# A block with 16,384 routed experts on one Trainium2 core: the expert outputs summed with the tokens on the partitions, in six banks held over all 128 tiles

## The chip, the cores and the metric

One core of a Trainium2 chip runs the whole program. The metric is device microseconds of one execution. The kernel before took 2893.17 us (median of three runs, 2893.05 to 2893.21). Five engines run beside each other, each in the order of its own queue: PE (matmuls; its weight loads are listed as PEld), DVE (vector work), ACT (activations and copies), POOL (here the gathers and some products) and SP (here it only issues DMAs). DMA issues stand in the queues of SP, ACT and POOL, and sixteen DMA engines carry them out.

## What is computed

The program is two transformer blocks on one sequence of 512 tokens, 1024 wide, in float32. The first ends in a mixture of 128 x 128 experts ("peer"), and the change lies wholly in that:

```python
def one_block(hb):                       # 128 tokens
    ...
    g = jax.nn.softmax(top_s, axis=-1)   # 8 heads x 16 chosen experts per token
    u = u_tab[idx]
    act = jax.nn.gelu(jnp.einsum('thkd,td->thk', u, hb))
    wts = (g * act.astype(jnp.float32)).astype(hb.dtype)
    v = v_tab[idx]
    return jnp.einsum('thk,thkd->td', wts, v)
```

Both expert tables are 16,384 x 1024. After this come a SwiGLU feed-forward (`f1`), a mixing layer and a second feed-forward.

## The kernel before

Activations lie transposed: eight tiles `x[m]` of 128 features by 512 tokens. Each float32 operand of a product is split into two fp32r parts, `hi` (a rounded copy, made by ACT) and `lo` (the rest, made by DVE), and a product is three matmuls: hi x hi, lo x hi, hi x lo (`mm3`, lines 235 to 237). Weights come through `wchunk`: SP loads 512 KB into one of three `wraw` buffers (line 210), ACT makes `whi` (line 211), DVE makes `wlo` (line 212), three buffers each. In the rows of a product the first name behind the arrow streams through the array, the second is loaded as weights.

The experts (`phase_b`) are computed in two ways. For the first 128 tokens the chosen rows are gathered: POOL issues an indirect DMA per slot (line 924, 128 of `u_nat` and 128 of `v_nat`, 512 KB each, four `row` buffers) and DVE multiplies and sums each row (lines 935 and 942). For the other 384 tokens (`ND`) all experts are computed densely, and a gate that is zero for experts not chosen weighs them. The gates, [12 blocks of 32 tokens, 128, 128, 32], are made with one-hot products on PE and written to DRAM in twelve writes by ACT's queue (line 884).

The dense part works on 128 tiles of 128 experts. `u_tile` multiplies one tile of `u` with the tokens, 24 matmuls of 384 columns, and applies the gelu (line 958). In the first stage, while the routing runs, 68 tiles are computed and written to DRAM (`spill`). The second stage, which the change rewrites, computes the other 60 `u` tiles and all v products. Its unit is a group of four tiles (`v_group`): read the gates of the group (line 989, runs of 512 bytes), read spilled tiles back (line 997), multiply by the gates (line 999; every second tile on POOL, the others on DVE), split into `whi__` and `wlo__` (lines 1002 and 1003), then for each of eight feature tiles m sum four tiles in one PSUM bank, 12 matmuls of 384 columns with the weights `pv` loaded and the weighted activations streaming, and add the bank to `x[m]` on DVE (line 1014). `seq` mixes the groups of spilled tiles and of tiles computed here; a group whose tiles are computed here starts right behind its fourth `u` tile. The last group also feeds `nf`, the norm ahead of the feed-forward (lines 135 to 147).

`weave` lets the gather run beside this at a set rate, and `pace` ties each of its steps to a recent matmul. A scheduler then sets the order within each engine's queue. PSUM has eight banks: two `mm`, two `S`, two `L`, one `T`, one `st`.

Of the kernel before, what the change touches and what calls it, by code (L numbers as in the profile page):

```python
# [7 lines left out]
F32 = mybir.dt.float32  # L8
F32R = mybir.dt.float32r
# [4 lines left out]
AF = mybir.ActivationFunctionType  # L14
OP = mybir.AluOpType
# [7 lines left out]
T = 512  # L23
# [27 lines left out]
GR = 0.45  # L51
RR = 1.1
VR = 0.345
AR = 1.4
MR = 1.75
PT = 12
SO = 0.5
TB = 8
BC = 2600
GSC = 32768.0  # L60
# [110 lines left out]
class Kern:  # L171
# [539 lines left out]
    def phase_b(self, n2):  # L711
        nc, I, x = self.nc, self.I, self.x
        ACT, V, G = nc.scalar, nc.vector, nc.gpsimd
        ND = T - TG
        NTB = ND // 32
        dp = self.ctx.enter_context(self.tc.tile_pool(name="dram", bufs=1, space=DRAM))
        Gd = dp.tile([NTB, 128, 128, 32], F32, name="gates")
        Sd = dp.tile([SPILL, 128, ND], F32, name="spill")
        eg = ExitStack()
        gp_ = eg.enter_context(self.pool("gath", "right"))  # L720
        er = ExitStack()
# [2 lines left out]
        rp = erq.enter_context(self.pool("route", "right"))  # L724
# [43 lines left out]
        rp = er.enter_context(self.pool("route2", "right"))  # L768
# [4 lines left out]
        spilled = {}  # L773
# [137 lines left out]
        def gather():  # L911

            g2 = gsel0.rearrange("p h s -> p (h s)")
            acc = gp_.tile([128, 1024], F32, name="gacc")
            V.memset(acc, 0.0)
            dots = gp_.tile([128, 128], F32, name="dots")
            junk = gp_.tile([128, 1024], F32, name="junk")
# [12 lines left out]
            for n, (tab, s) in enumerate(seq):  # L930
                if n + ROWB - 1 < len(seq):
                    issue(n + ROWB - 1)
                row = rows.pop(n)
                if tab == "u":
                    self.pace(V.scalar_tensor_tensor(junk, row, 1.0, hnat, op0=OP.mult, op1=OP.mult,  # L935
                                                     accum_out=dots[:, s:s + 1]), BACK)
                    if s % 16 == 15:
                        ss = slice(s - 15, s + 1)
                        ACT.activation(dots[:, ss], dots[:, ss], AF.Gelu_apprx_tanh)
                        V.tensor_tensor(dots[:, ss], dots[:, ss], g2[:, ss], op=OP.mult)  # L940
                else:
                    self.pace(V.scalar_tensor_tensor(acc, row, dots[:, s:s + 1], acc, op0=OP.mult, op1=OP.add), BACK)  # L942
                yield 1170
            for k in range(2):
                pt = self.ps("T")
                for q in range(4):
                    m = 4 * k + q
                    nc.tensor.transpose(pt[:, q * 128:(q + 1) * 128], acc[:, m * 128:(m + 1) * 128], self.ident)
                for q in range(4):
                    m = 4 * k + q  # L950
                    V.tensor_tensor(x[m][:, :TG], x[m][:, :TG], pt[:, q * 128:(q + 1) * 128], op=OP.add)
                yield 800

        def u_tile(j, pool, spill):
            ps = self.ps("mm")
            yield from self.proj_g(ps, I["u"][j], hhi, hlo, n=ND, cost=490)
            g = pool.tile([128, ND], F32, name="gs", bufs=3 if spill else 2 * GS)
# [4 lines left out]
            yield 0  # L962

        def u_spill():
            for j in range(SPILL):
                yield from u_tile(j, rp, True)

        gat = gather()

# [14 lines left out]
        ev = ExitStack()  # L984
        vp = ev.enter_context(self.pool("vph", "right"))

        def v_group(g, last):
            gt = vp.tile([128, NTB, GS, 32], F32, name="gt", bufs=2)
            nc.sync.dma_start(gt.rearrange("p a j t -> p a (j t)"),
                              Gd[:, :, g * GS:(g + 1) * GS, :].rearrange("a p j t -> p a (j t)"))  # L990
            W = []
            for q in range(GS):
                j = g * GS + q
                s = spilled[j]
                if s is None:
                    s = vp.tile([128, ND], F32, name="gr", bufs=4)
                    nc.sync.dma_start(s, Sd[j])
                s3 = s.rearrange("p (a t) -> p a t", t=32)
                (G if q % 2 else V).tensor_tensor(s3, s3, gt[:, :, q, :], op=OP.mult)
                a = vp.tile([128, ND], F32R, name="whi_", bufs=2 * GS)  # L1000
                c = vp.tile([128, ND], F32R, name="wlo_", bufs=2 * GS)
                ACT.activation(a, s, AF.Copy)
                V.tensor_tensor(c, s, a.bitcast(F32), op=OP.subtract)
                W.append((a, c))
            for mp in range(4):
                whi, wlo = self.wchunk(I["pv"][g, mp].rearrange("p m j d -> p (m j d)"), 1024)
                for m2 in range(2):
                    m = 2 * mp + m2
                    ps = self.ps("L" if m2 else "S")
                    for q in range(GS):  # L1010
                        o = slice((m2 * GS + q) * 128, (m2 * GS + q + 1) * 128)
# [3 lines left out]
                    if last:  # L1015
                        nf.add(m, x[m])

        nf = Norm(self, "f1")
        sg = list(range(SPILL // GS))
        ug = list(range(SPILL // GS, NG))  # L1020
        seq = []
        ns, nu = len(sg), len(ug)
        a = b = 0
        while a < ns or b < nu:
            if a < ns and (b >= nu or (a + SO) * nu <= b * ns):
                seq.append(sg[a])
                a += 1
            else:
                seq.append(ug[b])
                b += 1  # L1030

        def u_all():
            for g in ug:
                for q in range(GS):
                    yield from u_tile(g * GS + q, vp, False)

        def main():
            ugen = u_all()
            total = nu * GS * 9
            vsteps = NG * GS * 8  # L1040
            done, vdone = 0, 0
            for n, g in enumerate(seq):
                need = (ug.index(g) + 1) * GS * 9 if g in ug else 0
                while done < need:
                    yield next(ugen, 0)
                    done += 1
                if n == len(seq) - 1:
                    yield None
                for c in v_group(g, n == len(seq) - 1):
                    yield c  # L1050
                    vdone += 1
                    while done < total and done * vsteps < vdone * total * 1.08:
                        yield next(ugen, 0)
                        done += 1
            for c in ugen:
                yield c

        weave(main(), gat, VR)
        ev.close()
# [505 lines left out]
def layout(i):  # L1565

    f = lambda n: np.asarray(i[n])
# [33 lines left out]
    r["pv"] = c(f("peer_v")[0].reshape(NG, GS, 128, 4, 2, 128).transpose(0, 3, 2, 4, 1, 5))  # L1601
# [73 lines left out]
```

## Time and profile before

| what | value |
|---|---|
| median of the runs | 2893.17 us |
| profiled execution, its own time | 2896.98 us |
| its span in the trace | 2895.1 us |
| PE busy | 2808.9 us, 97% |
| DVE busy | 2019.7 us, 70% |
| ACT busy | 1159.6 us, 40% |
| POOL busy | 477.1 us, 16% |
| mean granted clock of PE | 0.983 of full speed |

The profiled execution is 3.8 us longer than the median. PE is busy nearly throughout, so a microsecond can come out of PE's own work, out of the gaps in it, or out of stretches at the lower of its two clocks. The second stage of the experts lies between 1101.0 us (the end of the last spilled `u` tile) and 1931.4 us (the end of the last v product), 830.4 us. DVE and the DMA engines are both about nine tenths busy there.

### The profile page before, as it was taken

What the parts mean: (1) busy time and instruction counts of PE and PEld (TensorE: products, weight loads), DVE (VectorE), ACT (ScalarE), POOL (GpSimd) and SP (SyncE); (2) the same over time, 40 slices, a digit from 0 to 9 for tenths busy, and PEclk for the clock granted to TensorE, in tenths of its full rate; (3) what the DMA queues carried; (4) which work ended last, traced back from release to release, by engine and by line L of the source; (5) the groups of instructions that cost most, each with busy time, mean ns of one, the idle gap of its engine ahead of it and who ended that gap; (6) DMA issues with size and microseconds to landing.
All of it is one profiled execution on the core that took longest, in us unless ns stands there. A gap on an engine that the chain in (4) does not pass through costs nothing. (4 is left out here: it accounts for less than half of the span.)

```text
span 2895.1 us, 38874 instructions
## 1 busy us (share of the span) xinstructions
PE 2808.9 (97%) x14613; PEld 2439.5 (84%) x14613; DVE 2019.7 (70%) x3960; ACT 1159.6 (40%) x1723; POOL 477.1 (16%) x352
## 2 busy tenths in 40 slices
PE   8999999999899998999999999999999999999999
PEld 6678777788798898999999999998888877688887
DVE  6753466679999997998898898974443467554432
ACT  5742344333365663333333333343322355633221
POOL 0000000000042334444444444400000000000000
PEclk9999999999999999999999999999999999899999
DMA  4223211332387889988988898832233321132232
GB/s 167 64 77 109 72 52 52 98 108 79 110 302 247 322 296 363 319 308 304 316 293 310 315 307 296 299 123 96 95 97 92 102 64 41 57 107 95 96 103 78
DMA packets 189564, 494.35 MB, mean 171 GB/s; under 512 B 16160, under 2 KB 84896, under 8 KB 187712
## 3 DMA queue, kind: packets, MB, share of 16 engines
q1 hardware_dynamic: 140672, 318.77, 33.2%
q0 software_dynamic: 36864, 134.23, 13.3%
q10 hardware_dynamic: 11840, 38.87, 3.5%
q8 instruction: 115, 1.88, 0.3%
q14 instruction: 73, 0.60, 0.1%
HBM read 450.84 MB, written 40.63 MB: 170 GB/s over the span
## 5 line engine op out<-in xcount | busy, mean ns | idle before, releaser
L211 ACT ACTIVATE whi<-wraw 128x1024 fp32r<-128x1024 f32 (+1 forms) x526 | 547.0, 1041 | 1249.3 <-PE mm L236 625.3
L237 PE MATMUL mm<-hhi,wlo 128*128 128x512 f32 (+1 forms) x2272 | 845.2, 372 | 34.7 <-DVE wlo L212 34.5
L235 PE MATMUL mm<-hhi,whi 128*128 128x512 f32 (+1 forms) x2272 | 855.5, 377 | 20.0 <-ACT whi L211 10.1
L236 PE MATMUL mm<-hlo,whi 128*128 128x512 f32 (+1 forms) x2272 | 842.5, 371 | 0.0
L212 DVE TENSOR_TENSOR wlo<-wraw,whi 128x1024 fp32r<-128x1024 f32 (+1 forms) x526 | 642.0, 1222 | 243.1 <-ACT whi L211 240.2
L237 PEld LDWEIGHTS mm<-hhi,wlo 128*128 128x128 f32 x2272 | 433.1, 191 | 93.0 <-DVE wlo L212 42.4
L235 PEld LDWEIGHTS mm<-hhi,whi 128*128 128x128 f32 x2272 | 433.6, 191 | 76.5 <-ACT whi L211 11.2
L236 PEld LDWEIGHTS mm<-hlo,whi 128*128 128x128 f32 x2272 | 433.4, 191 | 49.5 <-issue 3.1
L924 POOL DMA_INDIRECT row<-u_nat,eidx x128 | 190.9, 1491 | 588.4 <-PE mm L236 329.4
L924 POOL DMA_INDIRECT row<-v_nat,eidx x128 | 188.8, 1475 | 249.0 <-PE mm L237 58.7
L942 DVE SCALAR_TENSOR_TENSOR gacc<-row,dots,gacc 128x1024 f32<-128x1024 f32 x128 | 173.2, 1353 | 20.2 <-DMA row<-v_nat,eidx 10.7
L935 DVE SCALAR_TENSOR_TENSOR junk<-row,hnat 128x1024 f32<-128x1024 f32 x128 | 162.5, 1269 | 15.6 <-DMA row<-u_nat,eidx 9.0
L235 PE MATMUL mm<-fhi,whi 128*128 128x512 f32 x352 | 139.1, 395 | 0.0
L237 PE MATMUL mm<-fhi,wlo 128*128 128x512 f32 x352 | 139.0, 395 | 0.0
L236 PE MATMUL mm<-flo,whi 128*128 128x512 f32 x352 | 139.0, 395 | 0.0
L881 ACT ACTIVATE stg<-L 128x512 f32<-128x512 f32 x96 | 100.5, 1155 | 46.7 <-PE L L878 37.5
L1080 DVE TENSOR_TENSOR fu<-mm,nbc 128x512 f32<-128x512 f32 x40 | 27.6, 691 | 125.3 <-PE mm L237 125.3
L1076 DVE TENSOR_TENSOR fg<-mm,nbc 128x512 f32<-128x512 f32 x40 | 27.6, 691 | 84.2 <-PE mm L237 84.2
L1014 DVE TENSOR_TENSOR x<-x,L 128x384 f32<-128x384 f32 x128 | 70.0, 547 | 19.4 <-PE L L237 19.2
L237 PEld LDWEIGHTS mm<-fhi,wlo 128*128 128x128 f32 x352 | 66.0, 187 | 16.2
L235 PEld LDWEIGHTS mm<-fhi,whi 128*128 128x128 f32 x352 | 66.0, 187 | 16.2
L236 PEld LDWEIGHTS mm<-flo,whi 128*128 128x128 f32 x352 | 66.0, 187 | 16.0
(2390 smaller groups left out, 4790.9 us busy)
## 6 DMA issues: line engine op xcount, KB each, us to landing
wraw<-u SPq DMA_DIRECT2D x128, 512.0 KB
wraw<-pv SPq DMA_DIRECT2D x128, 512.0 KB
gates<-stg ACTq DMA_DIRECT2D x12, 2048.0 KB
gt<-gates SPq DMA_DIRECT2D x32, 768.0 KB
spill<-gs ACTq DMA_DIRECT2D x68, 192.0 KB
gr<-spill SPq DMA_DIRECT2D x68, 192.0 KB
wraw<-w_f1g SPq DMA_DIRECT2D x22, 512.0 KB
wraw<-w_f1u SPq DMA_DIRECT2D x22, 512.0 KB
```

What stands on the lines that cost most here:

```text
L211: nc.scalar.activation(hi[:, :n], raw[:, :n], AF.Copy)
L212: (nc.gpsimd if pool_lo else nc.vector).tensor_tensor(lo[:, :n], raw[:, :n], hi[:, :n].bitcast(F32), op=OP.subtract)
L235: nc.tensor.matmul(ps, a[0], b[0], start=start, stop=False)
L236: nc.tensor.matmul(ps, a[0], b[1], start=False, stop=False)
L237: self.mms.append(nc.tensor.matmul(ps, a[1], b[0], start=False, stop=stop).ins.name)
L881: ACT.activation(stg[:, :, o:o + 4].rearrange("p j t -> p t j"), gp.rearrange("p (t j) -> p t j", t=4), AF.Copy, scale=1.0 / GSC)
L924: self.pace(G.indirect_dma_start(out=rows[n], out_offset=None, in_=I[tab + "_nat"], in_offset=bass.IndirectOffsetOnAxis(ap=eidx[:, s:s + 1 ...
L935: self.pace(V.scalar_tensor_tensor(junk, row, 1.0, hnat, op0=OP.mult, op1=OP.mult, accum_out=dots[:, s:s + 1]), BACK)
L942: self.pace(V.scalar_tensor_tensor(acc, row, dots[:, s:s + 1], acc, op0=OP.mult, op1=OP.add), BACK)
L1014: V.tensor_tensor(x[m][:, TG:], x[m][:, TG:], ps[:, :ND], op=OP.add)
L1076: V.tensor_tensor(g, pg, n.bc, op=OP.mult)
L1080: V.tensor_tensor(u, pu, n.bc, op=OP.mult)
```

## The change

The v products are turned over. The weighted activations of a tile, in pieces of 128 tokens, are loaded as weights, and the rows of `v_nat`, 512 columns at a time, stream. A tile is then six sums (two halves of the features, three pieces of tokens) of three matmuls of 512 columns, 18 instead of 24 matmuls. The six sums stay in six banks (`Y`: `S`, `L`, `T`, `S`, `L`, `st`) over all 128 tiles, so that the adds to `x` of each group go. At the end the six banks are copied out, transposed in 24 pieces and added to `x`.

The tiles are taken in natural order. The spilled ones are the first four of every eight and the last four, 68 as before. Each tile is prepared (gate product, split) three tiles ahead of its v product, all on DVE and ACT; POOL keeps only the gathers. The gates are read for eight tiles at once, in four DMAs of three blocks each (runs of 1 KB), a group ahead. Six `u` tiles stand ahead of the first v product, and the others are spread one step at a time among the v products. The gather gets a fifth row buffer: its u step writes the product over the row, and `junk` goes. The last three tiles are taken half by half, so that the first half is done early.

```diff
-GS = 4
-NG = 128 // GS
-SPILL = 68
+T_ALL = 128
+GS = 8
+NG = T_ALL // GS
+PREP = 3
+LEAD = 48
+TAIL = 3
+WB, GTB = 8, 2
...
-ROWB = 4
+ROWB = 5
...
-                    self.pace(V.scalar_tensor_tensor(junk, row, 1.0, hnat, op0=OP.mult, op1=OP.mult,
+                    self.pace(V.scalar_tensor_tensor(row, row, 1.0, hnat, op0=OP.mult, op1=OP.mult,
...
-                (G if q % 2 else V).tensor_tensor(s3, s3, gt[:, :, q, :], op=OP.mult)
...
-                        self.mm3(ps[:, :ND], (whi[:, o], wlo[:, o]), W[q], q == 0, q == GS - 1)
-                        yield 490
-                    V.tensor_tensor(x[m][:, TG:], x[m][:, TG:], ps[:, :ND], op=OP.add)
...
+        def gates_in(g, part):
+
+            if part == 0:
+                gts[g] = vp.tile([128, NTB, GS, 32], F32, name="gt", bufs=GTB)
+            a = slice(part * NTB // 4, (part + 1) * NTB // 4)
+            nc.sync.dma_start(gts[g][:, a].rearrange("p a j t -> p a (j t)"),
+                              Gd[a, :, g * GS:(g + 1) * GS, :].rearrange("a p j t -> p a (j t)"))
...
+        def prep(j):
+
+            s = acts.pop(j)
+            s3 = s.rearrange("p (a t) -> p a t", t=32)
+            V.tensor_tensor(s3, s3, gts[j // GS][:, :, j % GS, :], op=OP.mult)
...
+            ACT.activation(a, s, AF.Copy)
+            V.tensor_tensor(c, s, a.bitcast(F32), op=OP.subtract)
...
+        Y = [[self.ps(t) for t in tags] for tags in (("S", "L", "T"), ("S", "L", "st"))]
+
+        def v_part(j, h, b):
+            a, c = W[j]
+            whi, wlo = chunks[j]
+            o, bs = slice(h * 512, h * 512 + 512), slice(b * 128, b * 128 + 128)
+            st, sp = j == 0, j == T_ALL - 1
+            y = Y[h][b]
+            nc.tensor.matmul(y, a[:, bs], whi[:, o], start=st, stop=False)
+            nc.tensor.matmul(y, a[:, bs], wlo[:, o], start=False, stop=False)
+            self.mms.append(nc.tensor.matmul(y, c[:, bs], whi[:, o], start=False, stop=sp).ins.name)
...
+        def y_add(m):
+            h, q = divmod(m, 4)
+            ps = self.ps("mm")
+            for b in range(3):
+                nc.tensor.transpose(ps[:, b * 128:(b + 1) * 128], yn[h, b][:, q * 128:(q + 1) * 128], self.ident)
+            V.tensor_tensor(x[m][:, TG:], x[m][:, TG:], ps[:, :ND], op=OP.add)
+            nf.add(m, x[m])
...
+            for part in range(4):
+                gates_in(0, part)
+            yield from u_to(48)
...
+                    for i in range(6):
+                        v_part(n, i // 3, i % 3)
+                        yield 680
+                        yield from u_to(int(len(here) * 8 * min(1.0, (n * 6 + i + LEAD) / (T_ALL * 6))))
```

SP's queue at the start of the second stage, before (`gt` are gates, `gr` a spilled tile read back, `wraw` a chunk of weights):

```order
L210 DMA wraw_10495<-u 128x1024
L210 DMA wraw_10534<-u 128x1024
L210 DMA wraw_10570<-u 128x1024
L210 DMA wraw_10606<-u 128x1024
L989 DMA gt_10641<-gates_5047 128x12x128
L210 DMA wraw_10663<-pv 128x1024
L210 DMA wraw_10700<-pv 128x1024
```

The same place now:

```order
L213 DMA wraw_10615<-u 128x1024
L1002 DMA gt_10498<-gates_5047 128x3x256 x4
L213 DMA wraw_10651<-u 128x1024
L213 DMA wraw_10687<-u 128x1024
L1008 DMA gr_10720<-spill_5048 128x384
L1008 DMA gr_10722<-spill_5048 128x384
L1008 DMA gr_10724<-spill_5048 128x384
L1008 DMA gr_10726<-spill_5048 128x384
L213 DMA wraw_10748<-v_nat 128x1024
```

In both, four loads of `u` stand ahead of the first gate read; the fifth and sixth, and the first spilled tiles, now stand behind it where two loads of `pv` stood.

PE's queue in the second stage before, from the last steps of a group's fourth `u` tile (`mm`) into the group's v products (`S`):

```order
L235 MATMUL mm_11103<-hhi_6145,whi_11105 128x384
L236 MATMUL mm_11103<-hlo_6146,whi_11105 128x384
L237 MATMUL mm_11103<-hhi_6145,wlo_11106 128x384
L235 MATMUL S_11167<-whi__11142,whi_11162 128x384
L236 MATMUL S_11167<-wlo__11143,whi_11162 128x384
L237 MATMUL S_11167<-whi__11142,wlo_11163 128x384
```

PE's queue now, around the end of one `u` tile (`mm_10940`) and the start of the next (`mm_11048`):

```order
L238 MATMUL mm_10940<-hhi_6145,whi_10942 128x384
L239 MATMUL mm_10940<-hlo_6146,whi_10942 128x384
L240 MATMUL mm_10940<-hhi_6145,wlo_10943 128x384
L1034 MATMUL L_10493<-whi_11026,whi__10888 128x512
L1035 MATMUL L_10493<-wlo_11027,whi__10888 128x512
L1036 MATMUL L_10493<-whi_11026,wlo__10889 128x512
L1034 MATMUL T_10494<-whi_11026,whi__10888 128x512
L1035 MATMUL T_10494<-wlo_11027,whi__10888 128x512
L1036 MATMUL T_10494<-whi_11026,wlo__10889 128x512
L238 MATMUL mm_11048<-hhi_5197,whi_11050 128x384
L239 MATMUL mm_11048<-hlo_5198,whi_11050 128x384
L240 MATMUL mm_11048<-hhi_5197,wlo_11051 128x384
```

A `u` tile stood in one piece of 24 matmuls in many places; now its eight steps are spread over about two v tiles, and its chunk keeps one of the three buffers for that long.

PE's queue now behind the last v product (`st_10497`): the transposes out of the copied banks (line 1054), with the feed-forward's first matmuls (`S_17257`) drawn between.

```order
L1036 MATMUL st_10497<-whi_17002,wlo__16944 128x512
L1054 MATMUL mm_17072<-consts_74,gt_17016 128x128 x3
L1054 MATMUL mm_17084<-consts_74,gt_17016 128x128 x3
L238 MATMUL S_17257<-hhi_17034,whi_17259 128x512
L239 MATMUL S_17257<-hlo_17035,whi_17259 128x512
L1054 MATMUL mm_17096<-consts_74,gt_17016 128x128 x3
L1054 MATMUL mm_17108<-consts_74,gt_17016 128x128 x3
L240 MATMUL S_17257<-hhi_17034,wlo_17260 128x512
```

Before, the feed-forward's first matmul stood directly behind the last v product.

## Rows read from the trace of the kernel before

**Rows 1.** Busy time by stretch: us, then engines (x instructions), PE clock, DMA share, GB/s.

```profile
1107.70:1118.00 10.30, 5.33 (x17) 5.33 (x18) 9.09 (x8) 0.00 (x0) 4.95 (x4) 0.50 1.06 377
1118.00:1146.00 28.00, 24.42 (x136) 23.14 (x134) 23.53 (x28) 10.91 (x17) 14.64 (x12) 1.00 1.05 363
1333.00:1336.40 3.40, 3.40 (x12) 3.40 (x12) 3.40 (x7) 1.44 (x2) 0.00 (x0) 0.50 1.01 309
1763.10:1769.90 6.80, 5.12 (x16) 4.62 (x16) 5.94 (x7) 0.92 (x1) 2.67 (x2) 0.50 1.04 360
1769.90:1931.40 161.50, 161.18 (x927) 160.37 (x927) 137.28 (x191) 63.16 (x87) 50.56 (x39) 1.00 0.70 242
```

**Rows 2.** Matmuls in order, start and duration in us, at the lower clock.

```profile
1112.67 0.69 PE L237 MATMUL mm<-hhi,wlo 128*128 128x384 f32 x1 [7.19 <-DVE wlo L212]
1113.15 0.53 PE L235 MATMUL mm<-hhi,whi 128*128 128x384 f32 x1
1113.47 0.53 PE L236 MATMUL mm<-hlo,whi 128*128 128x384 f32 x1
```

**Rows 3.** PE's waits from 1146 us to 1931.4 us: us in total, times, longest.

```profile
PE S L237 <- DVE wlo L212: 5.5, 4, 3.0
PE mm L237 <- DVE wlo L212: 3.9, 2, 2.6
PE S L235 <- ACT whi__11157 L1002: 1.3, 1, 1.3
...
PE S L235 <- ACT whi__13831 L1002: 0.3, 1, 0.3
```

**Rows 4.** DVE in order of time, with the idle time before each and its releaser.

```profile
1108.47 1.28 DVE L942 SCALAR_TENSOR_TENSOR gacc<-row,dots,gacc 128x1024 f32<-128x1024 f32 x1 [3.18 <-DMA row<-v_nat,eidx]
1326.87 1.85 DVE L999 TENSOR_TENSOR gr<-gr,gt 128x384 f32<-128x384 f32 x2 [4.63 <-DMA gt<-gates]
1757.93 0.56 DVE L999 TENSOR_TENSOR gr<-gr,gt 128x384 f32<-128x384 f32 x1 [2.59 <-DMA gr<-spill]
```

**Rows 5.** The waits of SP's queue: us in total, times, longest.

```profile
SPq L989 <- DMA gates<-stg: 12.6, 1, 12.6
```

**Rows 6.** Matmuls of the attention's value projection, half a chunk streaming, 24 apart.

```profile
260.43 0.39 PE L235 MATMUL S<-whi,hhi 128*128 128x512 f32 x1
...
265.87 0.39 PE L235 MATMUL S<-whi,hhi 128*128 128x512 f32 x1
```

**Rows 7.** Matmuls of the first feed-forward's down projection, 24 apart.

```profile
2200.25 0.39 PE L235 MATMUL mm<-fhi,whi 128*128 128x512 f32 x1
...
2205.85 0.39 PE L235 MATMUL mm<-fhi,whi 128*128 128x512 f32 x1
```

**Rows 8.** DVE, 1146 to 1931.4 us, by line: busy us, mean ns, idle before.

```profile
L212 DVE TENSOR_TENSOR wlo<-wraw,whi 128x1024 fp32r<-128x1024 f32 x182 | 234.8, 1294 | 19.0 <-ACT whi L211 17.8 <-issue 0.4
L942 DVE SCALAR_TENSOR_TENSOR gacc<-row,dots,gacc 128x1024 f32<-128x1024 f32 x99 | 134.1, 1355 | 11.5 <-PE mm L237 5.7 <-PE L L237 3.5 <-DMA row<-v_nat,eidx 2.0
L1014 DVE TENSOR_TENSOR x<-x,S 128x384 f32<-128x384 f32 x125 | 68.3, 546 | 5.4 <-PE S L237 5.1
L1014 DVE TENSOR_TENSOR x<-x,L 128x384 f32<-128x384 f32 x124 | 67.8, 547 | 19.4 <-PE L L237 19.2
L999 DVE TENSOR_TENSOR gs<-gs,gt 128x384 f32<-128x384 f32 x28 | 15.4, 550 | 0.0
```

**Rows 9.** ACT, the same stretch and columns.

```profile
L211 ACT ACTIVATE whi<-wraw 128x1024 fp32r<-128x1024 f32 x180 | 190.8, 1060 | 367.3 <-PE L L236 232.3 <-PE mm L236 70.2 <-DMA wraw<-u 11.0
```

**Rows 10.** All engines, 1895 to 1935 us, by line, the same columns.

```profile
L136 DVE SCALAR_TENSOR_TENSOR hlo<-x,vecs,hhi 128x512 fp32r<-128x512 f32 x7 | 5.2, 746 | 0.8 <-ACT hhi L135 0.8
...
L147 DVE TENSOR_TENSOR acc<-acc,sq 128x512 f32<-128x512 f32 x6 | 4.1, 683 | 0.0
```

**Rows 11.** A copy of a full bank, by line 497: count, duration ns min/median/max.

```profile
L497 DVE COPY kraw<-mm x8: 691/692/693, 302.1 to 446.3; 128x512 f32<-128x512 f32 x8
```

**Rows 12.** Four transposes of 128 x 128 on PE, start and duration in us.

```profile
1885.51 0.60 PE L948 MATMUL T<-consts,gacc 128*128 128x128 f32 x4
```

More of the change, by code (lines that the diff above doesn't have):

```diff
@@ L717, in phase_b @@
         Gd = dp.tile([NTB, 128, 128, 32], F32, name="gates")
[L718 removed]
+        Sd = dp.tile([T_ALL, 128, ND], F32, name="spill")
         eg = ExitStack()
@@ L962, in u_tile, with slot @@
             yield 0
+        def slot(j):
+            return j % GS < GS // 2 or j >= T_ALL - GS // 2
         def u_spill():
-            for j in range(SPILL):
-                yield from u_tile(j, rp, True)
+            for j in range(T_ALL):
+                if slot(j):
+                    yield from u_tile(j, rp, True)
         gat = gather()
@@ L1018, in phase_b @@
-        nf = Norm(self, "f1")
[L1019 to L1027, printed above, removed]
-            else:
[L1029 to L1035, printed above, removed]
+        order = list(range(T_ALL))
@@ new lines, in phase_b, with act_in @@
+        here = [j for j in order if not slot(j)]
+        gts, acts, W, chunks = {}, {}, {}, {}
+        def gates_in(g, part):
[4 more added lines that the diff above has]
+                              Gd[a, :, g * GS:(g + 1) * GS, :].rearrange("a p j t -> p a (j t)"))
+        def act_in(j):
+            if slot(j):
+                acts[j] = vp.tile([128, ND], F32, name="gr", bufs=7)
+                nc.sync.dma_start(acts[j], Sd[j])
@@ new lines, in prep, with chunk @@
+        def prep(j):
+            s = acts.pop(j)
+            s3 = s.rearrange("p (a t) -> p a t", t=32)
+            V.tensor_tensor(s3, s3, gts[j // GS][:, :, j % GS, :], op=OP.mult)
+            a = vp.tile([128, ND], F32R, name="whi_", bufs=WB)
+            c = vp.tile([128, ND], F32R, name="wlo_", bufs=WB)
+            ACT.activation(a, s, AF.Copy)
+            V.tensor_tensor(c, s, a.bitcast(F32), op=OP.subtract)
+            W[j] = a, c
+        def chunk(j):
+            chunks[j] = self.wchunk(I["v_nat"][j * 128:(j + 1) * 128], 1024)
@@ new lines, in phase_b, with y_out @@
+        yn = {}
+        def y_out(h, b):
+            if not yn:
+                yn["t"] = vp.tile([128, NTB, GS, 32], F32, name="gt", bufs=GTB)
+            t = yn["t"].rearrange("p a j t -> p (a j t)")[:, (3 * h + b) * 512:(3 * h + b + 1) * 512]
+            if (h + b) % 2:
+                V.tensor_copy(t, Y[h][b])
+            else:
+                ACT.activation(t, Y[h][b], AF.Copy)
+            yn[h, b] = t
+        def y_add(m):
[5 more added lines that the diff above has]
+            nf.add(m, x[m])
@@ L1037, in main, with u_all @@
         def main():
+            def u_all():
+                for j in here:
+                    yield from u_tile(j, vp, False)
+                    acts[j] = spilled[j]
             ugen = u_all()
[L1039 to L1049, printed above, removed]
-                    yield c
[L1051 to L1054, printed above, removed]
@@ L1055, in main, with u_to @@
-            for c in ugen:
-                yield c
+            done = [0]
+            def u_to(n):
+                while done[0] < n:
+                    c = next(ugen, None)
+                    if c is None:
+                        return
+                    done[0] += 1 if c else 0
+                    yield c
+            n_v = T_ALL - TAIL
+            for part in range(4):
+                gates_in(0, part)
+            yield from u_to(48)
+            loaded = prepped = 0
+            for n in range(n_v + 1):
+                if n < n_v:
+                    g = 1 if n < GS - PREP else (n + PREP) // GS + 1
+                    part = n - 1 if n < GS - PREP else (n + PREP) % GS
+                    if 0 <= part < 4 and g < NG:
+                        gates_in(g, part)
+                    last = T_ALL if n == n_v - 1 else min(n + PREP + 1, T_ALL)
+                    while loaded < min(T_ALL, last + 4):
+                        act_in(loaded)
+                        loaded += 1
+                    while prepped < last:
+                        j = prepped
+                        if not slot(j):
+                            yield from u_to((here.index(j) + 1) * 8)
+                            for c in ugen_end(ugen, j):
+                                yield c
+                        prep(j)
+                        prepped += 1
+                if n < n_v:
+                    chunk(n)
+                    for i in range(6):
+                        v_part(n, i // 3, i % 3)
+                        yield 680
+                        yield from u_to(int(len(here) * 8 * min(1.0, (n * 6 + i + LEAD) / (T_ALL * 6))))
+                    del chunks[n]
@@ new lines, in main @@
+            tail = list(range(n_v, T_ALL))
+            yield None
+            for h in range(2):
+                for j in tail:
+                    if h == 0:
+                        chunk(j)
+                    for b in range(3):
+                        v_part(j, h, b)
+                        yield 680
+                    if h == 1 and j < tail[-1]:
+                        m = j - n_v
+                        y_add(m)
+                for b in range(3):
+                    y_out(h, b)
@@ L1058, in phase_b, with ugen_end @@
+            for m in range(TAIL - 1, 4):
+                y_add(m)
+            for m in range(4, 8):
+                y_add(m)
+        def ugen_end(g, j):
+            while j not in acts:
+                c = next(g, None)
+                yield c or 0
         weave(main(), gat, VR)
```

35 lines of the change are left out of this document (3 added, 32 removed).

## The prediction

> **What bounds the kernel now.** I read the busy table first, then PE by stretches, then who ended each of its waits. PE is busy 97% of the span, so time can leave the kernel in three ways only: fewer or shorter matmuls, gaps in PE's row closed, or stretches at the lower clock (granted 0.50, that is 1.2 GHz) brought up to 2.4. The reader is to see in [rows 1] that all three exist in the second stage of the experts: at its end 161.18 of 161.50 us are matmul, while 1118 to 1146 us has 3.6 us of gaps and three stretches run at half clock. [rows 3] name what ended the later waits: wlo of a chunk, made by DVE, and whi__ of the activations, made by ACT. [rows 4] show why DVE was late: it stood behind DMAs, 4.63 us for gates and 2.59 us for a spilled tile, with the next chunk's wlo queued behind.
>
> **The change part by part.** The sum is made against the profiled execution, 2896.98 us; the median is 3.8 us lower.
>
> 1. *The products.* At the end of the stage a matmul of 384 columns takes 161.18 / 927 = 0.174 us [rows 1] (the last row); 128 tiles x 24 are 3072, or 534.5 us. Now 128 x 18 = 2304 of 512 columns. The nearest row of the same make (a chunk streams, activations are loaded) is the value projection: (265.87 - 260.43) / 24 = 0.2267 us [rows 6], so 522.3 us: **-12.2**. The columns are equal (3072 x 384 = 2304 x 512); what is saved is what a matmul costs beside its columns. The other bound is the down projection with 0.2333 us [rows 7]: 537.5 us, a loss of 3.0. I take the first, since its operands lie as those here do.
>
> By the Trainium skill (TensorE: Matmul & The Clock Gate, Back-to-back issue gap) the gap of a single warm matmul is N/2.4 GHz plus a fixed 2.5 ns; for a long stream it names 131 ns at 512 columns, far below what [rows 6] show. By the formula, an estimate, the two shapes take 162.5 and 215.8 ns, hence 499.2 and 497.3 us: the turned products would give 2 us instead of 12.2. The rows stand 11 ns above the formula in both shapes and so bear the rule out badly.
>
> 2. *The start of a group.* Eleven such waits for whi__, from 1.3 to 0.3 us (the first and the last in [rows 3]), sum to 10.7 us: PE waits there for ACT's split of tiles whose gate product came late. Tiles are now split three ahead, some 18 us of PE's work (three times 18 x 0.2267 us, with 11 u matmuls of 0.174 us to a tile). ACT needs little, so nothing is late next: **-10.7**.
>
> 3. *The gaps at 1118 to 1146.* 28.00 - 24.42 = 3.6 us [rows 1]. They are of the same making, the first groups being prepared while PE waits: **-3.6**.
>
> 4. *DVE late behind DMAs.* From 1146 us on PE waits 5.5 and 3.9 us for wlo [rows 3], and next to these waits stand 3.40 and 5.12 us of matmul at granted clock 0.50 [rows 1]. A matmul there takes 0.32 us (1113.15 to 1113.47, [rows 2]) and not 0.174, so 46% of 8.52 us, 3.9 us, is lost as well. Gates are now asked for a group ahead and spilled tiles four tiles ahead, both over 20 us, against DVE's 4.63 and 2.59 us behind them [rows 4]; without the gaps that stand ahead of those stretches the clock has no cause there to fall: **-13.3** (9.4 + 3.9).
>
> 5. *DVE and POOL.* 256 adds to x at 0.547 us [rows 8] go, 140 us. The 64 gate products that POOL did come to DVE at 0.55 us [rows 8], 35 us. DVE's queue gets 105 us lighter on balance, of 729 us busy. It isn't the bound, so that is worth nothing itself; it is the cover for step 7.
>
> 6. *The start, about 1105 to 1113 us.* PE waits 7.19 us for the first wlo [rows 2]; DVE stands behind a gathered row, 3.18 us [rows 4]; SP's first gate read waits 12.6 us for the last gates written [rows 5], and in both orders the same four u loads stand ahead of it. What changes is the row buffers, five for four, and that u loads five and six now stand behind that read, where v chunks stood. I take **0**. Were the wait gone with its half clock (5.33 us at 0.50 [rows 1], 46% of it 2.4 us), that would be -9.6. The six tiles ahead promise a cover of six; only four are loaded when SP stops.
>
> 7. *Added: buffers held.* A u tile, in one piece so far, is spread over about two v tiles, and its chunk keeps one of three whi and wlo buffers for as long. Through the other two pass the v chunks, and a new chunk needs ACT's 1.06 us [rows 9] and DVE's 1.29 us [rows 8], 2.35 us, between the last reading of a buffer and the first reading of its next content. In the changed order PE has only 1.2 to 2.1 us of other work between these at some 27 places, about one per tile computed here. Before there were a dozen places of 1.75 us, and few show any wait. No buffer is let go earlier than before, so there is no gain below 0; from above a DVE operation of 1.3 us [rows 8] ahead at each: 27 x 1.3 = 35 us. I take **+6**, a quarter of a microsecond each, near the rows of before: there too the conversion overlaps PE's reading, since the parts are read one after the other.
>
> 8. *Added: rows and gates.* By the steps' weights a v step of 0.68 us now advances the gather by 0.335 x 680 / 1170 rows, 0.286 a microsecond; before one of 0.522 us by 0.345 x 490 / 1170, 0.277. Its last row stands some nine chunks ahead of the end, so nothing waits for it. Gate reads move the same bytes in runs twice as long, which can't cost more engine time. The DMA engines stay at nine tenths. A row that comes late holds DVE as in [rows 4]: **+3** for one such stop, from 0 to 6.
>
> 9. *Added: the tail.* 24 transposes at 0.60 us for four [rows 12] are 3.6 us, some of that the last one's tail: **+3**. Behind the last product stand a bank's copy, 0.69 us [rows 11], and for six of the eight x tiles an add (0.55 us), hlo (0.746) and the square's sum (0.683 us, [rows 10]), 12.6 us of DVE up to the last hlo that the feed-forward needs. PE has about 38 matmuls of the feed-forward (8.6 us) and 18 transposes (2 us) meanwhile: **+3**, from 0 (DVE's order lets hlo pass the sums) to 8.
>
> Sum: -12.2 - 10.7 - 3.6 - 13.3 + 6 + 3 + 3 + 3 = **-24.8**. 2896.98 - 24.8 = 2872.2 for a profiled execution, less 3.8: **2868 us** for the median.
>
> **The rivals.**
>
> *Everything goes.* The first wait too is gone: the fifth row buffer keeps DVE from standing behind a row, -9.6; steps 7 and 8 cost nothing, -9; the tail's wait is covered, -3. 2868 - 21.6 = 2847 us. For it speaks DVE's relief, against it [rows 5]: SP's stop isn't touched.
>
> *The products give nothing.* They take 0.2333 us each [rows 7], +15.2, and step 7 costs 12 instead of 6: 2868 + 21 = 2889 us. Within the measurement's reach of 2893. For it speaks that the stage streams weights that DVE and ACT have just written, with both at work; against it that [rows 6] do so too.
>
> *A matmul costs its columns and no more.* What [rows 1, 6] show beside them would belong to the streams and not to the count of matmuls; then step 1 gives 2 us, 2878 us.
>
> This is what the page's rule above comes to.
>
> *Slower: a chunk's conversion at each change of u tile.* If DVE, in the order of its queue, has a gathered row (1.36 us, [rows 8]) or another wlo ahead of the one that is wanted, the chain is 1.06 + 1.29 + 1.29 = 3.6 us against a cover of about 1.7, so 1.9 us at each of 27 places: 51 us, 2868 - 6 + 51 = 2913 us. Such stops could also lower the clock, as they do in [rows 1]. It decides from (24.8 + 6) / 27 = 1.1 us a place on. For it: DVE was 0.9 busy in this stage, so something stands ahead often. Against it: 105 us of DVE's work go, and the waits for wlo in [rows 3] are six in all.
>
> *It doesn't do what it says.* The six tiles ahead are four, as step 6 has it; a longer wait of SP for the gates would then stop all loads. That gives between 0 and +5 and lies inside the forecast.
>
> **How the numbers follow.** Forecast (2858 to 2880): 0.52. Everything goes (2847 to 2858): 0.18. Columns alone: 0.05. The products give nothing (2882 to 2899): 0.13. Slower: 0.12. What the measurement tells from no change is about 0.2%, 5.8 us: faster below 2887.4. Of the fourth case about four in five lie within 0.2%, so same has 0.11 and faster 0.52 + 0.18 + 0.05 + 0.02 = 0.77; slower 0.12. The range reaches from 2847 to 2889: below, all that can go is gone; above, the products' other bound. Outside lie the slower case, some of the fourth and a little below, together 2 in 10.
>
> **What would show it.** Step 1: v matmuls 0.227 us apart in a quiet stretch; 0.233 would be the fourth case, 0.230 half of it. Step 2: no wait of PE for whi__. Steps 3 and 4: DVE not idle behind gates or spilled tiles, and no stretch at granted clock 0.50 after 1146 us. Step 6: PE's wait of 7 us at the stage's beginning, again beside SP's wait for the gates. Step 7: waits of PE for wlo or whi of a chunk, and whether they stand at the changes of u tile; 6 us in all bears me out, 30 the slower case. Step 9: the gap between the last v product and the feed-forward. The stage, 830.4 us before, should take about 800 up to its last product, and the rest some 6 us more than before. I would be wrong first by step 7, whose 27 places the trace of before shows only by a dozen milder ones, and next by step 1, where 6.6 ns of a matmul decide 15 us.

## The result, and the profile after

The changed kernel takes 2923.48 us (median of four runs, 2920.85 to 2924.6) against 2893.19 us: 1.0091 times as long, 95% interval 1.0072 to 1.011. The forecast was 2868 us, faster; it was the other way, by about as much. The profiled execution has a span of 2919.1 us, 24.0 us more than before. Up to the last v product it is 20.9 us late (1952.3 us against 1931.4), behind it 3.1 us.

The stretches of PE, columns as in [rows 1]: the start, three of seven short stretches at half clock, the quiet end, and the stage as a whole.

```profile
1104.20:1114.40 10.20, 6.18 (x19) 6.18 (x20) 9.41 (x8) 0.00 (x0) 3.90 (x3) 0.50 0.96 359
1206.60:1210.00 3.40, 3.08 (x8) 2.51 (x9) 3.40 (x7) 0.00 (x0) 0.00 (x0) 0.50 0.68 210
1315.80:1319.20 3.40, 2.92 (x7) 2.43 (x8) 3.18 (x5) 0.53 (x1) 0.00 (x0) 0.50 1.02 403
1489.90:1496.70 6.80, 5.74 (x15) 5.05 (x16) 5.26 (x6) 0.07 (x1) 0.00 (x0) 0.50 0.74 256
1912.00:1942.00 30.00, 30.00 (x130) 24.14 (x130) 10.37 (x13) 8.25 (x9) 0.00 (x0) 1.00 0.39 123
1101.00:1952.30 851.30, 808.53 (x3734) 692.31 (x3735) 601.11 (x767) 281.58 (x388) 247.52 (x202) 0.98 0.84 290
```

PE is idle for 851.30 - 808.53 = 42.8 us of the stage, 30.4 before. 41 us of it run at half clock, in eight stretches, with 34.1 us of matmul in them; before it was 20.5 us in three, with 13.9 us (5.33 + 3.40 + 5.12, [rows 1]). PE's waits from 1146 us on, to be held against [rows 3] (us in total, times, longest):

```profile
PE mm L240 <- DVE wlo L215: 18.9, 6, 5.3
PE S L1035 <- DVE wlo L215: 13.5, 6, 4.5
```

The eleven waits for whi__ are gone, as forecast. The waits for wlo have grown from 9.4 to 32.4 us. Why DVE is late stands in DVE's own waits over the same stretch:

```profile
DVE gr L1014 <- DMA gt<-gates: 45.8, 13, 6.4
DVE gr L1014 <- DMA gr<-spill: 12.0, 9, 3.7
```

Before, gates held DVE up twice in the whole stage. Now they do so about once a group of eight tiles. One of these places, DVE's row first, SP's next, PE's last (`gr` are spilled tiles read back, `gs` tiles computed here):

```profile
1187.59 0.55 DVE L1014 TENSOR_TENSOR gs<-gs,gt 128x384 f32<-128x384 f32 x1
...
1197.25 1.22 DVE L215 TENSOR_TENSOR wlo<-wraw,whi 128x1024 fp32r<-128x1024 f32 x1
1203.08 1.50 DVE L1014 TENSOR_TENSOR gr<-gr,gt 128x384 f32<-128x384 f32 x3 [4.62 <-DMA gt<-gates]
1204.50 1.22 DVE L937 SCALAR_TENSOR_TENSOR row<-row,hnat 128x1024 f32<-128x1024 f32 x1
1205.64 0.08 DVE L937 DVE_READ_ACCUMULATOR row<-row,hnat 128x1 f32 x1
1205.64 1.22 DVE L215 TENSOR_TENSOR wlo<-wraw,whi 128x1024 fp32r<-128x1024 f32 x1
```

```profile
1188.16 2.00 SPq L1002 DMA_DIRECT2D gt<-gates  x3
1192.02 0.34 SPq L213 DMA_DIRECT2D wraw<-v_nat  x1
1192.41 0.48 SPq L1002 DMA_DIRECT2D gt<-gates  x1
```

```profile
1202.11 0.33 PE L239 MATMUL mm<-hlo,whi 128*128 128x384 f32 x1
1206.92 0.80 PE L1035 MATMUL S<-wlo,whi__11127 128*128 128x512 f32 x1 [4.47 <-DVE wlo L215]
1207.51 0.63 PE L1036 MATMUL S<-whi,wlo__11128 128*128 128x512 f32 x1
```

SP asks for the gates at 1188 to 1192 us. DVE comes to three products (`gr`) that need them at 1198.5, 6 to 10 us later, stands for 4.62 us, and the wlo that PE wants is behind them in DVE's queue. PE waits 4.47 us and runs at granted clock 0.50 afterwards. The tiles of these products are 24 to 26, and PE is at tile 12: the products stand 12 to 14 tiles ahead of their use.

The places in the queues say the same. This is for the fourth group (tiles 24 to 27), counted in v chunks that stand ahead (loads in SP's queue, splits in DVE's; a chunk is loaded some time before it is split). The last three rows are kernels of the experiments below.

| kernel | gates read | products of the spilled tiles |
|---|---|---|
| as changed | 13 13 13 14 | 12 12 12 14 |
| products tied | 14 14 14 16 | 22 23 23 25 |
| products tied loosely | 13 13 13 14 | 18 19 20 21 |
| third gate buffer | 7 8 8 8 | 8 14 14 14 |

SP can't read the gates earlier than that: their buffer is that of the group two before, and it comes free with that group's last product. That is the `gs` at 1187.59 us, and the read follows at 1188.16.

The second loss is in the products themselves. Two v matmuls in the quiet end, 18 apart:

```profile
1924.89 0.40 PE L1034 MATMUL L<-whi,whi__16756 128*128 128x512 f32 x1
1929.09 0.40 PE L1034 MATMUL L<-whi,whi__16796 128*128 128x512 f32 x1
```

4.20 / 18 = 0.2333 us, the value of [rows 7] and not that of [rows 6], with DVE and ACT about a third busy and the DMA engines at 0.39.

### The profile page after: what moved, and what is told of

Same layout as the page of the kernel before. It is cut to its first block, busy times and chain, and to the rows that moved or that the text cites. A ratio compares the mean times of both kernels' runs of the same rounds, so it can differ in the third digit from the quotient of the medians.

```text
span 2919.1 us, 37080 instructions
## 1 busy us (share of the span) xinstructions
PE 2820.8 (97%) x13869; PEld 2343.7 (80%) x13869; DVE 1901.8 (65%) x3779; ACT 1159.0 (40%) x1726; POOL 374.5 (13%) x288
## 5 line engine op out<-in xcount | busy, mean ns | idle before, releaser
L215 DVE TENSOR_TENSOR wlo<-wraw,whi 128x1024 fp32r<-128x1024 f32 (+1 forms) x526 | 629.0, 1197 | 301.3 <-ACT whi L214 299.5
L926 POOL DMA_INDIRECT row<-u_nat,eidx x128 | 185.0, 1445 | 691.5 <-PE mm L239 327.9
L926 POOL DMA_INDIRECT row<-v_nat,eidx x128 | 177.5, 1387 | 366.7 <-PE mm L240 86.9
L944 DVE SCALAR_TENSOR_TENSOR gacc<-row,dots,gacc 128x1024 f32<-128x1024 f32 x128 | 163.9, 1280 | 47.7 <-PE mm L240 13.4
L937 DVE SCALAR_TENSOR_TENSOR row<-row,hnat 128x1024 f32<-128x1024 f32 x128 | 156.0, 1220 | 51.1 <-PE mm L240 24.7
L239 PEld LDWEIGHTS mm<-flo,whi 128*128 128x128 f32 x352 | 66.0, 187 | 16.2
L240 PEld LDWEIGHTS mm<-fhi,wlo 128*128 128x128 f32 x352 | 66.0, 187 | 16.2
L1014 DVE TENSOR_TENSOR gr<-gr,gt 128x384 f32<-128x384 f32 x68 | 35.2, 553 | 60.5 <-DMA gt<-gates 45.8
```

The source lines that it names most:

```text
L215: (nc.gpsimd if pool_lo else nc.vector).tensor_tensor(lo[:, :n], raw[:, :n], hi[:, :n].bitcast(F32), op=OP.subtract)
L239: nc.tensor.matmul(ps, a[0], b[1], start=False, stop=False)
L240: self.mms.append(nc.tensor.matmul(ps, a[1], b[0], start=False, stop=stop).ins.name)
L937: self.pace(V.scalar_tensor_tensor(row, row, 1.0, hnat, op0=OP.mult, op1=OP.mult, accum_out=dots[:, s:s + 1]), BACK)
L1014: V.tensor_tensor(s3, s3, gts[j // GS][:, :, j % GS, :], op=OP.mult)
```

## The experiments

The kernel before was run beside each; its medians there were 2895 to 2898 us, with single runs from 2885 to 2905, so what counts is the ratio to it on the same chip. The ratios below are to its time, with the 95% interval behind them.

**The tie.** One line: the gate product waits for a recent matmul.

```diff
-            V.tensor_tensor(s3, s3, gts[j // GS][:, :, j % GS, :], op=OP.mult)
+            self.pace(V.tensor_tensor(s3, s3, gts[j // GS][:, :, j % GS, :], op=OP.mult), 6)
```

> The gate product of each tile is tied to the v matmul two sums of three before it, so that DVE's queue holds it about three tiles ahead of use and no longer ten to thirteen. Theory A (DVE stops for gates that were asked for only some 12 us before, because the buffer came free so late): DVE's 46 us of idle time before a gr product, ended by a gate DMA, falls below 10 us; PE's waits for wlo in the stage fall from 40 to about 15 us, the stretches at granted clock 0.50 from 41 to about 17 us; 2923 falls to about 2888 us. Rival B (chunk buffers held by spread u tiles cause the waits): waits for wlo stay near 40 us, 2918 to 2928 us. Rival C (gate transfers themselves are slow under load and would be late wherever they are wanted): 2910 to 2920 us.

Measured: 0.9933 (0.9909 to 0.9957), 2877.95 us. Its stage, its only waits of PE of a microsecond or more before the last v product, and DVE's only wait for a DMA:

```profile
1101.00:1911.70 810.70, 797.86 (x3755) 686.65 (x3754) 608.79 (x768) 290.94 (x390) 253.75 (x204) 0.99 0.87 306
```

```profile
PE mm L240 <- DVE wlo L215: 7.2, 1, 7.2
PE mm L238 <- ACT gs L960: 5.7, 1, 5.7
```

```profile
DVE gacc L944 <- DMA row<-v_nat,eidx: 7.2, 3, 5.1
```

The waits for gates and spilled tiles are gone altogether, and the stage is 40.6 us shorter. The u tiles are spread as before, and no wait stands at their changes: rival B falls. The same bytes move by the same four reads: rival C falls. PE's waits for wlo in the stage fell from 39.8 to 7.2 us where 15 were expected, half clock from 41 to 13.7 us where 17 were, and the kernel to 2878 us where 2888 were.

The same kernel again:

> The tied products once more, for comparison on the same chip: 0.993 of the kernel before, waits of PE only at the stage's start.

Measured: 0.9943 (0.9923 to 0.9962). It repeats.

**The tie, loosened** (`48` for `6` in the same line).

> The tie is loosened: a gate product may stand up to some eight tiles ahead of its v product (it stands about 6 ahead in DVE's queue, against 3 tied closely and 10 untied). Theory A counts time from the release of a gate buffer to the first product that wants the gates: some four tiles more than untied, 25 us, against waits of 3 to 6 us, so all but a few us of DVE's idle time behind gates goes: 2878 to 2886 us. If what counts is only that the products stand near their use (DVE's order, not the gates' time), it falls half way, 2895 to 2905 us.

Measured: 0.9932 (0.9909 to 0.9956). Six tiles ahead is as good as two. DVE waits for gates once, 5.4 us. So it is time between read and product that was missing, and not nearness to the use: in the fourth group the products stand six to eight tiles later than in the changed kernel, in later groups fewer.

**Gates read once.**

```diff
-            V.tensor_tensor(s3, s3, gts[j // GS][:, :, j % GS, :], op=OP.mult)
+            V.tensor_tensor(s3, s3, gts[0][:, :, j % GS, :], op=OP.mult)
...
-                    if 0 <= part < 4 and g < NG:
-                        gates_in(g, part)
```

> The gates of the first eight tiles are read once and used for all 128, so fifteen of sixteen gate reads are left out (the sums come out with wrong gates, the work of the engines is the same). Theory A: no wait of DVE for gates, PE's waits for wlo about 15 us, half clock about 17 us, 2885 to 2892 us, as with the tied products. Rival B: 2915 to 2925 us. Rival C: 2885 to 2892 us here, but 2910 to 2920 with the tied products.

Measured: 0.9989 (0.997 to 1.0007), 2893.73 us, above the 2885 to 2892 of theory A. It is better than the changed kernel by 1%, but worse than the tie, which reads all gates. The products, which the scheduler still puts far ahead, now stand behind the next read, that of the spilled tiles; DVE's row:

```profile
DVE gr L1014 <- DMA gr<-spill: 34.8, 23, 3.3
```

All three accounts had missed that. Without the gates' reads (60 of 384 KB) the wait moves on; with the order mended it goes.

**A third gate buffer,** without a tie.

```diff
-WB, GTB = 8, 2
+WB, GTB = 6, 3
...
-            g = pool.tile([128, ND], F32, name="gs", bufs=3 if spill else 8)
+            g = pool.tile([128, ND], F32, name="gs", bufs=3 if spill else 6)
...
-                acts[j] = vp.tile([128, ND], F32, name="gr", bufs=7)
+                acts[j] = vp.tile([128, ND], F32, name="gr", bufs=5)
```

> No tie; a third buffer for the gates (its room from six buffers for activations instead of eight, five for spilled tiles instead of seven, six for u tiles instead of eight). The gate reads no longer wait for the buffer of the group two before and stand some six v chunks further ahead in SP's queue; the products stay hoisted. Theory A: DVE's idle time behind gates falls from 52 to below 10 us, but the hoisted products then stand behind spilled tiles, 20 to 35 us as with gates read once; 2888 to 2900 us. Rival (a hoisted product is late whatever is done to the gates): about 50 us behind gates still, 2915 to 2925 us.

Measured: 1.0129 (1.0094 to 1.0164), 2933.72 us: slower than the changed kernel, and outside both forecasts. DVE's waits:

```profile
DVE gr L1014 <- DMA gr<-spill: 89.2, 38, 7.0
DVE gs L1014 <- DMA gt<-gates: 7.4, 1, 7.4
```

The gates are early now, as expected, and the spilled tiles are late far beyond the expected 20 to 35 us. SP's reads of them wait 109 us, in 43 stops, for the split that frees a buffer; in the changed kernel it was 11.7 us in 7, and with gates read once, with seven buffers still, 65.4 us in 33. So these buffers bind once the gates don't. With the tie SP waits 91.6 us for them too, but nothing comes late by it, as the products stand late as well. How much of the 89.2 us is due to five of them where there were seven was not separated.

**The spacing of matmuls** by the place of their operands. The edit, its core:

```diff
+            def run(s, l, n, times=48):
+                ps = self.ps("mm")
+                for i in range(times):
+                    nc.tensor.matmul(ps[:, :n], l[:, :128], s[:, :n], start=i == 0, stop=i == times - 1)
...
+            for n in (512, 384, 128):
+                run(low, mid, n)
+                run(low, big[20], n)
+                run(big[20], low, n)
+                run(big[20], big[28], n)
...
```

`whi` lies at 23 KB of a partition (not at 35, as the expectation has it), `hhi` at 59, `nbc` at 91 and 93, `za` at 103, `zc` at 111, `zg` at 127, `zu` at 183, the other `z` at 215 KB, by the program's allocation.

> Added at the start of the program: runs of 48 matmuls of one shape, with the streamed and the loaded operand at chosen places in a partition of SBUF (35 KB, 59 KB, 91 to 215 KB); the rest is the changed kernel, some 200 us longer. Theory D (a matmul of 512 columns costs 6 ns more where one of its operands lies in the upper half of a partition): 227 ns with both at 35 and 59 KB, 233 ns with either at 183 KB, and at 384 columns 174 ns in all cases; the step lies somewhere between 93 and 119 KB. Rival E (the 6 ns come from what else the stage does, DVE, DMA or the six banks): 227 ns in all cases of 512.

The rows are runs of 48 matmuls (96 with `nbc`, two places), with start and length in us; the first name streams. It is one execution; the granted clock is 1.00.

```profile
45.42 11.35 PE L303 MATMUL mm<-whi,zu 128*128 128x512 f32 x48
56.62 11.37 PE L303 MATMUL mm<-zu,whi 128*128 128x512 f32 x48
67.82 11.07 PE L303 MATMUL mm<-zu,z}_113 128*128 128x512 f32 x48
78.73 8.49 PE L303 MATMUL mm<-whi,hhi 128*128 128x384 f32 x48
87.06 8.64 PE L303 MATMUL mm<-whi,zu 128*128 128x384 f32 x48
95.54 8.50 PE L303 MATMUL mm<-zu,whi 128*128 128x384 f32 x48
103.88 8.51 PE L303 MATMUL mm<-zu,z}_113 128*128 128x384 f32 x48
...
133.61 22.01 PE L303 MATMUL mm<-whi,nbc 128*128 128x512 f32 x96
155.46 11.36 PE L303 MATMUL mm<-whi,za 128*128 128x512 f32 x48
166.66 11.36 PE L303 MATMUL mm<-whi,zc 128*128 128x512 f32 x48
```

From start to start of these rows, at 512 columns: one operand low and one high takes (56.62 - 45.42) / 48 = 0.2333 us, whichever of the two it is; both high (78.73 - 67.82) / 48 = 0.2273; both low, up to `nbc`, (155.46 - 133.61) / 96 = 0.2276. The step lies between 95 KB (the end of `nbc`) and 103 KB. At 384 columns it is (87.06 - 78.73) / 48 = 0.1735 for both low, (103.88 - 95.54) / 48 = 0.1738 with the streaming operand high, and (95.54 - 87.06) / 48 = 0.1767 with the loaded one high. DVE did next to nothing there, and each run of 48 went into one bank. Theory D holds, but for two things: what counts is whether the operands lie on one side, not that one is high; and 384 columns aren't quite free of it.

**The operands on one side.** Activations low, in three buffers, without and with the tie:

```diff
-            a = vp.tile([128, ND], F32R, name="whi_", bufs=WB)
-            c = vp.tile([128, ND], F32R, name="wlo_", bufs=WB)
+            w = self.wp.tile([128, 1024], F32, name="wraw", bufs=RAWB)
+            a, c = w[:, :ND].bitcast(F32R), w[:, ND:2 * ND].bitcast(F32R)
```

(and `raw` of a chunk from the pool `vp` in this stage).

> The split activations whi__ and wlo__ lie in the low buffers of wraw (23 to 35 KB) and the raw chunks of this stage high; three instead of eight buffers for the activations. Theory D: a v matmul takes 227 instead of 233 ns, 14 us less over 2304 of them, 2909 us if three buffers are enough; up to 2920 if not. Rival E: 233 ns as before, 2923 us or more.

Measured: 1.0144 (1.012 to 1.0167), 2938.84 us, above the 2909 to 2920 of theory D. A v matmul takes 230.2 ns on the mean, where the changed kernel's takes 232.6: 2.4 of the 6 ns come back where all engines work. The rest of the kernel loses more than that. At the start PE waits 16.2 us, as in the next run; and behind it 43.0 us for wlo (32.4 in the changed kernel), with DVE 59.8 us behind gates (45.8). What made the gates later still was not separated. No wait of PE is for the activations.

> The tie, and the split activations in three low buffers (chunks low too). If three buffers are enough now that DVE doesn't stop for gates: 230 ns a v matmul as in the untied form, 2304 x 2.4 ns = 5.5 us less than the tie alone, about 0.992 of the kernel before; if they aren't, waits for whi__ of the activations above 6 us and nothing gained.

Measured: 0.9944 (0.9926 to 0.9961), 230.1 ns. No wait for whi__ of the activations, so three buffers are enough. The gain of 5.8 us is given back at the two ends: at the start one wait is longer,

```profile
PE mm L240 <- ACT whi L216: 17.1, 1, 17.1
```

(7.2 and 5.7 us with the tie alone), since SP's stop for the gates now stands ahead of three loads of u,

```profile
1084.65 16.79 SPq L1005 DMA_DIRECT2D gt<-gates  x3
1101.54 1.79 SPq L215 DMA_DIRECT2D wraw<-u  x3
```

and behind the last v product the feed-forward starts after 6.9 us instead of 1.4. That its chunks stand there behind the last activations in the shared buffers is likely, but was not tried by itself.

The chunks of v high instead, two buffers each, with the tie (`WB` 5, `gr` 5, `ROWB` 4 for room):

```diff
-            chunks[j] = self.wchunk(I["v_nat"][j * 128:(j + 1) * 128], 1024)
+            raw = self.wp.tile([128, 1024], F32, name="wraw", bufs=RAWB)
+            hi = vp.tile([128, 1024], F32R, name="vhi", bufs=2)
+            lo = vp.tile([128, 1024], F32R, name="vlo", bufs=2)
...
```

> As the tied products, and the split chunks of v lie in two high buffers each (the activations lie high too); to make room five buffers for the activations instead of eight, five for spilled tiles instead of seven, four rows instead of five. By the measured placement rule (227 ns with both operands on one side, 233 with one on each) a v matmul falls from 232.6 to 227 to 230 ns, 6 to 13 us less than the tied products on the same chip, if two buffers are enough; rival: the two buffers bring waits for wlo of 5 us or more and eat it.

Measured: 1.0083 (1.0064 to 1.0101), 229 ns a v matmul. It falls on the rival's side: PE waits for the two buffers,

```profile
PE S L1041 <- DVE vlo L1027: 15.5, 16, 3.1
PE S L1040 <- ACT vhi L1026: 8.8, 6, 2.3
```

and half clock is back at 34 us.

**The start, and a better version.** The tie, and:

```diff
+            for c in u_to(24):
+                yield 0
             yield from u_to(48)
```

> The tie, and the gather isn't advanced during the first three u tiles of the stage, so that fewer gathered rows stand between the first splits of chunks on DVE. If the wait of 7 us at the stage's start comes from rows asked for in this stage, it goes, and with it up to 6 us (half clock too); if it comes from the rows that the first stage has left in DVE's queue, it stays at 7 us, 0.994 of the kernel before.

Measured: 0.9911 (0.9885 to 0.9938). The long wait stays,

```profile
PE mm L240 <- DVE wlo L215: 7.9, 1, 7.9
```

so by the expectation the rows that hold DVE up there are those that the first stage left in its queue. PE's waits of 3.4 to 5.7 us for a gelu, in the runs with a tie alone, are gone.

The loose tie and this together:

> The loose tie and the gather held for three u tiles together. The first leaves PE waiting 8 and 3 us at the stage's start, the second about 8; if they only take away the same waits, 0.991 to 0.993 of the kernel before, as each alone; if their small gains add, 0.990.

Measured: 0.9906 (0.9886 to 0.9925), 2870.72 us: the best of all, though not set apart from either alone. It beats both kernels.

The changed kernel again:

> The changed kernel as it is, on the same chip as the run beside it: 1.009 of the kernel before again, 1.017 to 1.019 of the tied one; if the difference between the chips has a part in the result, 1.005 or less.

Measured: 1.0088 (1.0063 to 1.0112) on that same chip. The result doesn't hang on the chip.

## Why the prediction was wrong

**Step 4 failed, and turned round.** It put the gates' lead over the products that want them at over 20 us, being asked for a group ahead; it was 6 to 10 us at the place above. The code is written so; but step 4 read only one end of the distance. A product's place in DVE's queue is the scheduler's, which put the gate products of spilled tiles, from the third group on, 8 to 14 tiles ahead of use (the last tile 7), right behind the read, and two buffers bind the read to the products of two groups before. DVE's queue, looked up at this place as SP's and PE's were, would have shown it: the reads at chunk 13, the products at chunk 12. Forecast -13.3; what came is +23 us of waits for wlo (32.4 for 9.4) and the half clock behind them. The tie shows the cause: with the products two to three tiles ahead, no wait for wlo and no half clock is left from 1146 us to the last v product, which is all that step 4 forecast; with some six tiles ahead it is the same.

**Step 1 was mis-sized,** +1.4 us instead of -12.2 (2304 x 0.2326, the mean of the stage, against 3072 x 0.174). [rows 6] were taken "since its operands lie as those here do". They don't: in [rows 6] both lie low, in [rows 7] and here the activations lie above the step at 95 to 103 KB and the chunks below. The two bounds were the two cases of one rule, and only the wrong reason for choosing stood between them. The formula of the Trainium skill (TensorE: Matmul & The Clock Gate, Back-to-back issue gap) gives 215.8 ns at 512 columns as an estimate, and with it a gain of 2 us for this step. The measured 227 and 233 ns both stand above it. That its 2 us come nearer to the measured loss of 1.4 us than the forecast did is chance.

**Step 7 was too dear.** No wait stands at a change of u tile once DVE doesn't stop: 0 instead of +6, and the slower rival, 51 us by that mechanism, gave the right sign by the wrong one. Its condition (1.1 us a place) was never near. The 27 places aren't "about one per tile computed here" either: 54 of the 60 tiles are spread, so it is one for two of them.

**What held.** Step 2: no wait for whi__ is left, -10.7. Step 5: DVE's busy time in the stage falls by 128 us (729.15 to 601.11; 105 forecast). Step 6: PE's wait is 7.4 us for 7.2, SP's first gate read waits 15.6 us for 12.6, and nothing is gained, as taken. Step 8: the last row ends at 1904.5 us, 48 us ahead of the last product, and from 1146 us on DVE doesn't wait for a row, 0 instead of +3. Step 9: 3.1 us instead of 6; the changed kernel's second profile is longer there by another 2.9 us, so this term isn't set apart from nothing. **Step 3** didn't come: from 1118 to 1146 us PE is idle for 28.00 - 24.99 = 3.0 us, 3.6 before. The old gaps are gone, and PE now waits for a gelu there. That stands in ACT's queue behind the splits of u loads five and six, which step 6 saw moved behind the gate read and took at nothing:

```profile
1118.00:1146.00 28.00, 24.99 (x127) 22.27 (x126) 22.03 (x29) 12.47 (x20) 7.56 (x7) 1.00 1.04 390
```

```profile
1122.43 1.06 ACT L214 ACTIVATE whi<-wraw 128x1024 fp32r<-128x1024 f32 x1 [6.75 <-DMA wraw<-u]
1124.23 1.06 ACT L214 ACTIVATE whi<-wraw 128x1024 fp32r<-128x1024 f32 x1 [0.74 <-DMA wraw<-u]
1125.19 0.47 ACT L960 ACTIVATE gs<-mm 128x384 f32<-128x384 f32 x1
```

```profile
1125.72 0.44 PE L238 MATMUL mm<-hhi,whi 128*128 128x384 f32 x1 [2.22 <-ACT gs L960]
```

**The account.** The stage is 20.9 us longer: 12.4 us of idle time (42.8 - 30.4), 9.3 us of half clock (46% of the 20.2 us of matmul more in it), 1.4 us of products; 2.2 us the other way aren't placed. The tied kernel's span is 2875.7 us, 19.4 less than before: idle time -17.6 (12.8 for 30.4), half clock -2.5 (46% of 8.5 less 13.9 us), products +1.4; 0.7 us aren't placed. That it is only 5 us from the sum of the forecast is in part luck: step 1 fell short by 13.6 us, and the new wait for a gelu, 5.7 us there with half clock behind it, stands where step 3 had -3.6; against that the 15 us that steps 7 to 9 added didn't come.

What stays open: how much of the wait in the run with a third gate buffer is due to the fewer buffers for spilled tiles, and whether the 5 to 8 us that 230.2 to 229 ns are worth (2304 matmuls, 2.4 to 3.6 ns less each) can be had without losing them elsewhere.

## What to carry to other kernels

A read that is asked for early isn't early where the instruction that wants it was put early as well: compare both places in the two queues, for each engine whose queue holds something that PE waits for. A product that waits for a DMA belongs as late in its engine's queue as its use allows, since everything behind it waits too; a tie to a recent matmul did here in one line what fewer reads or more buffers didn't. Where two rows differ by a few per cent for the same shape, find out what the difference is before choosing one of them.

## What the runs showed of the hardware

A matmul of 512 fp32r columns takes 227.3 to 227.6 ns with both operands below 95 KB or both above 183 KB of their partitions, and 233.3 ns with one on each side; the step is between 95 and 103 KB. At 384 columns it shows only with the loaded operand high and the streaming one low (176.7 ns; 173.5 to 173.8 in the other cases). With DVE, ACT and the DMA engines at work the gain is smaller: 230.1 ns with both low, 229 with both high. In the changed kernel, from 1146 us to the last v product, seven stops of PE of 2.7 to 5.3 us each went with 3.4 or 6.8 us at granted clock 0.50, which began within about 1 us of the stop's end. The seven stops are 27.3 us; the 27.9 us of matmul in those stretches lost, by an estimate (46% of it, from [rows 2] and [rows 1]), some 13 us more.
